# A streamed expert layer: single pieces early in the weight ring, and the second expert's first chunks ahead of the transposes

## The chip, the cores and the metric

The kernel runs on one core of one Trainium2 chip. The metric is the time of one execution on the device in microseconds (us); it is measured in several runs, of which the median is given. The profile is of one further execution.

## The reference

One layer of a streaming encoder on 512 frames of width 2048, in float32. The first part (norm, combined projection, chunked attention, short convolution, output projection) gives x. The second part, where the change lies, is a mixture of experts with hard routing:

```
glog, elog = xt @ w_rg + b_rg, xt @ w_re + b_re     # 4 groups, 32 experts in all
g_sel = argmax(glog);  top_v, top_i = top_k(elog of that group, 2)
w_tok = softmax(glog)[g_sel] * softmax(top_v)
...
a = silu(xblk @ w_gate[e]) * (xblk @ w_up[e])       # 2048 -> 512, for each expert e
y[tokens of e] += w_tok * (a @ w_down[e])           # 512 -> 2048
...
return rmsnorm(x + y, norm_final)
```

Every expert has 12.6 MB of weights (gate and up 8.4, down 4.2), 403 MB for all 32, and each is used once, by the few dozen tokens that picked it.

## The kernel before

**First part.** Up to about 800 us TensorE works through the dense projections and the attention; weights of the first two experts are fetched meanwhile. Then each token picks its experts (`choose`, `rank`), the experts are ordered by their number of tokens, and lists of token numbers are made.

**Units.** Experts are handled in units that share 128 slots: the first unit has the two experts with most tokens (by place in that order), 64 slots each; then a unit of four experts with 32 slots (a quarter unit); one full unit of two experts with 64 slots; two heavy units, whose first expert has 64 + 32 slots and whose second has 32; eight more full units; and a last quarter unit. For each unit the rows of its tokens are fetched from DRAM into one buffer, `xrow`, by an indirect DMA of POOL (L680), and turned by four steps (`turn_rows`, L687: four transposes each and a multiplication on DVE) into `xg`.

**One expert.** `gate_up` (L764) multiplies the slots with eight chunks of gate and up weights, accumulating in PSUM. `act1` (L773, L774; L778 to L782 for 32 slots) makes the activation on ACT and DVE, `act2` transposes it on TensorE (L788) and copies it (L790). `down` (L802) is the projection back with four chunks, whose results ACT and DVE write as a high and a low half, Yh and Yl (L808, L809).

**Combines.** The results of a unit go back to the token rows by multiplication with the unit's slot table. `slot_t` (L823) transposes the table; `comb` (L831, L832) are the 16 combines of a unit, each followed by an addition on DVE (L833). They stand in a list, `todo`, from which the next unit takes pieces to fill TensorE while its own work waits: 16 combines and then the four turns of the next unit's rows. How many are taken where is written in `plan`: a tuple for after each chunk of `gate_up`, then `gap` (ahead of the transposes of `act2`), `aft` (behind them) and `mid` (inside `down`). TensorE's order is as written; the other engines are ordered by the framework.

**The ring.** Weights pass through 14 places of 1 MB (`RING`). `loads` lists all pieces in order; `pump(n)` says that n more pieces will have been used and issues loads on the SP queue (L488, in `load_e`) for the places that this gives back. Before, two pieces are loaded by one DMA of 2 MB, except the last eight; such a load waits until both places are free. The order of the loads is that of use:

```
loads = [(u[i][0], c) for u in units for g in groups(u) for cs in (range(8), range(8, 12)) for i in g for c in cs]
```

**The first unit** is special: while its two `gate_up` run, `first(c)` and `second(c)` do the rest of the routing ahead of chunk c: fetching the rows for the second half of `xg`'s columns (`fetch_first`), picking rows by products with a selection (`first_gather`), counting and routing weights (`counts`, `weights`).

Of the kernel before, what the change touches and what calls it, by code (L numbers as in the profile page):

```python
# [10 lines left out]
F32 = mybir.dt.float32  # L11
# [8 lines left out]
P = 128  # L20
S = 512
# [8 lines left out]
SLOT = 64  # L30
NOV = 16
RING = 14
# [19 lines left out]
def tile_hymba_moe_layer(ctx, tc, xr, xT, smalls, wr, b3, wv, wt, wo, wgu, wd, out):  # L52
    nc = tc.nc

    def pool(stack, name, bufs=1, space=None, side="left"):
        kw = dict(name=name, bufs=bufs, reuse_waits="tile", side=side)
        if space is not None:
            kw["space"] = space
        return stack.enter_context(tc.tile_pool(**kw))
# [127 lines left out]
    fill = []  # L187
# [162 lines left out]
    for hb in range(4):  # L350
        us, ys = [], []
        ps = proj_t(8 + hb, FR)
        for c in range(2):
            u = ap.tile([P, S], F32, name="u", tag="u", bufs=2)
# [115 lines left out]
    chunks = {}  # L470
# [175 lines left out]
    for c, pl, tag, n in ((6, ylp, "Yl", 1), (7, wk, "xg", 2)):  # L646
        w = pl.tile([P, D], F32, name="w", tag=tag, bufs=n)
# [6 lines left out]
    psX = pool(ctx, "psX", space=PSUM)  # L654
# [17 lines left out]
    Sm = wk.tile([P, NT, 2 * SLOT], F32, name="Sm", tag="Sm", bufs=2)  # L672
    xg = wk.tile([P, KT, 2 * SLOT], F32, name="xg", tag="xg", bufs=2)
# [4 lines left out]
    def fetch_rows(ix, w):  # L678

        nc.gpsimd.indirect_dma_start(out=xrow[0:w, :], out_offset=None, in_=xd[:, :],  # L680
                                     in_offset=bass.IndirectOffsetOnAxis(ap=ix, axis=0),
                                     bounds_check=S - 1, oob_is_err=False)
# [14 lines left out]
    def token_of(dst, src, w):  # L697

        e = eye2[:, 0:NE]
        nc.vector.tensor_scalar(e[:, 0:w], src, 0.0, NONE, ALU.is_equal, ALU.mult)  # L700
        nc.vector.scalar_tensor_tensor(dst, src, -1.0, e[:, 0:w], ALU.add, ALU.add)
# [35 lines left out]
    def fetch_first():  # L737

        idp = psX.tile([P, 1], F32, name="idp", tag="dn", bufs=2)
        for t in range(NT):  # L740
            nc.tensor.matmul(idp, Sm[:, t, :], tok[:, t:t + 1], start=t == 0, stop=t == NT - 1)
        token_of(idx[:, 0:1], idp, 1)
        fetch_rows(idx[:, 0:1], P)
# [3 lines left out]
    def run(n):  # L747
        for _ in range(min(n, len(todo))):
            todo.pop(0)()

    def gate_up(xg, blocks, ch, fill, pre=None):
        pss = [psX.tile([P, S], F32, name="gu", tag="gx", bufs=3) for _ in blocks]
        for c in range(8):
            w = ch[c].rearrange("p (j g f) -> p j g f", j=2, g=2)
            if pre is not None:
                pre(c)
            for (n, o, _), ps in zip(blocks, pss):
                for j in range(2):  # L760
                    for g in range(2):
                        r = 64 * g if n == SLOT else 64 * j + 32 * g
                        q = 2 * c + j if n == SLOT else c
                        nc.tensor.matmul(ps[r:r + n, :], xg[:, 2 * c + j, o:o + n], w[:, j, g, :],  # L764
                                         start=q == 0, stop=q == (KT - 1 if n == SLOT else 7))
            run(fill if isinstance(fill, int) else fill[c])
        return pss
# [17 lines left out]
    def act2(n, a):  # L785
        tp = psM.tile([P, 4, n], F32, name="mp", tag="cb", bufs=3)
        for f in range(4):
            nc.tensor.transpose(tp[:, f, :], a[:, P * f:P * f + P], ident[0:n, 0:n])  # L788
        aT = wk.tile([P, 4, n], F32, name="aT", tag="aT", bufs=2)
        nc.scalar.copy(aT, tp)  # L790
        return aT
# [27 lines left out]
    def slot_t(Sm, w):  # L819

        tp = psM.tile([w, S], F32, name="mp", tag="cb", bufs=3)
        for t in range(NT):
            nc.tensor.transpose(tp[:, P * t:P * t + P], Sm[:, t, :], ident)  # L823
        ST = bt.tile([w, S], F32R, name="ST", tag="x1T", bufs=2)
        nc.vector.tensor_copy(ST, tp)  # L825
        return ST

    def comb(ST, Yh, Yl, w, t, db):
        sl = slice(S * db, S * db + S)
        cb = psM.tile([P, S], F32, name="cb", tag="cb", bufs=3)  # L830
        nc.tensor.matmul(cb, ST[:, P * t:P * t + P], Yh[0:w, sl], start=True, stop=False)  # L831
        nc.tensor.matmul(cb, ST[:, P * t:P * t + P], Yl[0:w, sl], start=False, stop=True)  # L832
        nc.vector.tensor_tensor(ACC[:, t, sl], ACC[:, t, sl], cb, ALU.add)  # L833

    def comb_units(Sm, Yh, Yl, w):
        box = []
        us = [lambda: box.append(slot_t(Sm, w))]
        for db in range(4):
            for t in range(NT):
                us.append(lambda t=t, db=db: comb(box[0], Yh, Yl, w, t, db))  # L840
        return us
# [115 lines left out]
    def first(c):  # L957
        if c in (4, 6):
            turn_rows(xg, P, 2 * c)
        if c == 1:  # L960
            fetch_first()
            for t in range(1, NT):
                first_gather(xps[1:2], 4, t)
        if c == 2:
            box["cntc"] = counts()
            box["rhs"] = weights()
        if c == 6:
            by_place(box["cntc"])
# [159 lines left out]
    def full(c, o):  # L1128
        return c, [(SLOT, o, c)]
# [8 lines left out]
    units = [[full(0, 0), full(1, SLOT)], Q[0], N[0], Hv[0], Hv[1]] + N[1:] + [Q[1]]  # L1138
# [7 lines left out]
    loads = [(u[i][0], c) for u in units for g in groups(u) for cs in (range(8), range(8, 12)) for i in g for c in cs]  # L1146
    loads = loads[:6] + loads[8:]

    loads[-8:] = [(u[0], c) for c in range(8, 12) for u in units[-1][2:]]
    regs = {}  # L1150

# [2 lines left out]
    def pump(n):  # L1154

        used[0] += n
        while nload[0] < len(loads):
            m = nload[0]
            w = 2 if m < len(loads) - 8 else 1
            if used[0] < m + w - RING:  # L1160
                break
            pos, c = loads[m]
            if pos < 2:
                e = slice(pos, pos + 1)
            else:
                if pos not in regs:
                    regs[pos] = nc.sync.value_load(ctl[0:1, pos:pos + 1], min_val=0, max_val=NE - 1)
                e = bass.ds(regs[pos], 1)
            chunks.setdefault(pos, []).extend(load_e(part(e, c, w), w))
# [4 lines left out]
    prev = []  # L1174
# [5 lines left out]
    def rcol(c):  # L1180
        return WRv[:, 1, c:c + 1]
# [17 lines left out]
    def step(p):  # L1199
        nonlocal cur, prev  # L1200
        Sm, xg, gu_ = cur
        cur = None
        todo.extend(prev)
        if p:
            cur = rows(p + 1)
            todo.extend([lambda g=cur[2], n=n: gather_to(g, n + 1) for n in range(4)])
        if p == 1:
            for j in range(len(HEAVY)):
                todo.insert(-4 * j - 2, lambda j=j: order_heavy(j))
        Yh, Yl = ytile()  # L1210

        def pre(c):
            gather_to(gu_, min(4, (c + c % 2) // 2 + 1))


        if p == 0:
            plan = [(0, 0, 0, 0)] * 2
        elif len(units[p]) == 4:
            plan = [(1, 0, 0, 0), (1, 3, 0, 0), (1, 2, 1, 0), (1, 2, 1, 0)]
        else:  # L1220
            plan = [((2, 2, 2, 2, 2, 2, 1, 1), 2, 0, 0), (1, 0, 0, 0)]
        turns = groups(units[p])
        left = len(units[p])
        for turn in turns:
            acts = []
            for i in turn:
                e, blocks = units[p][i]
                if p == 0:
                    pss = ps_first[i]
                    if i:  # L1230
                        order()
                        cur = rows(1)
                else:
                    pss = gate_up(xg, blocks, chunks[e], plan[i][0], pre)
                pump(8 if p or i else 6)
                acts.append([act1(n, ps, rcol(c)) for (n, _, c), ps in zip(blocks, pss)])
            for i, act in zip(turn, acts):
                e, blocks = units[p][i]
                _, gap, aft, mid = plan[i]
                left -= 1  # L1240
                if p == 0 and i:
                    gather_to(cur[2], 4)
                if left == 0:
                    gap = max(gap, len(todo) - aft - mid)
                run(gap)
                aTs = [act2(n, a) for (n, _, _), a in zip(blocks, act)]
                run(aft)
                if left == 0:
                    prev = comb_units(Sm, Yh, Yl, 2 * SLOT)
                    prev.pop(0)()  # L1250
                down([(n, o, aT, wcol(n, c)) for (n, o, c), aT in zip(blocks, aTs)], chunks[e], Yh, Yl, mid)
                pump(4)
        run(len(todo))
# [180 lines left out]
```

## Time and profile before

| what | value |
|---|---|
| median of 3 runs | 1802.97 us (1799.13 to 1803.94) |
| profiled execution | 1804.06 us, span 1802.4 us |
| TensorE busy | 1672.7 us (93%) |
| DVE, ACT, POOL busy | 770.6, 483.4, 81.2 us |
| mean granted TensorE clock | 0.966 of full |
| moved by DMA | 505.51 MB, mean 280 GB/s |

The span is the time from the first to the last instruction. Busy shares are means over stages with different limits; a TensorE that is busy is not at its peak, because matmuls overlap. A wait is given with what ended it.

### The profile page before, as it was taken

To read this page: it belongs to the slowest core of one execution; us is meant where nothing else is said; L and a number is where in the kernel's file an instruction comes from. 1 tells how busy PE (TensorE), PEld (TensorE's weight loads), DVE (VectorE), ACT (ScalarE), POOL (GpSimd) and SP (SyncE) were. 2 spreads that over 40 slices of the span, in tenths; PEclk is the share of its full clock that TensorE was granted. 3 is DMA by queue.
4 is the path that set the end of the run, shared out by engine and by line. 5 is a ranking of instruction groups with operands and counts; after the bars stand their busy time and mean duration, and the time that the engine had idled before them with its cause. 6 is when DMAs were issued, how large, how long until landed. Compare 5 with 4: busy or idle time off the path is not lost. (4 is left out here: it accounts for less than half of the span.)

```text
span 1802.4 us, 22250 instructions
## 1 busy us (share of the span) xinstructions
PE 1672.7 (93%) x9034; PEld 1012.6 (56%) x9034; DVE 770.6 (43%) x1427; ACT 483.4 (27%) x887; POOL 81.2 (5%) x91
## 2 busy tenths in 40 slices
PE   9999999999999999999876998889999999999974
PEld 7887777778888788774432333334444444443321
DVE  5236556542343633253543344443343334333446
ACT  6235555532222412330222112211111111111213
POOL 0000000011211200010000000000000000000000
PEclk9999999999999999989988999999999999999986
DMA  8222222232222635247999999899999999999995
GB/s 341 101 94 82 94 82 94 77 117 96 104 104 94 237 148 208 96 187 277 391 426 427 426 429 390 358 428 427 426 427 427 427 425 419 427 425 411 426 424 219
DMA packets 48187, 505.51 MB, mean 280 GB/s; under 512 B 6224, under 2 KB 6352, under 8 KB 12368
## 3 DMA queue, kind: packets, MB, share of 16 engines
q1 hardware_dynamic: 44784, 491.45, 66.8%
q0 software_dynamic: 3296, 12.59, 1.8%
q8 instruction: 73, 1.20, 0.3%
q14 instruction: 34, 0.28, 0.0%
HBM read 501.91 MB, written 8.39 MB: 283 GB/s over the span
## 5 line engine op out<-in xcount | busy, mean ns | idle before, releaser
L116 DVE TENSOR_TENSOR wlo<-raw,whi 128x1024 fp32r<-128x1024 f32 x126 | 159.1, 1266 | 281.1 <-ACT whi L115 280.3
L232 PE MATMUL pp<-hTh,whi 128*128 128x512 f32 x640 | 255.1, 399 | 0.0
L232 PE MATMUL pp<-hTl,whi 128*128 128x512 f32 x640 | 250.5, 391 | 0.0
L232 PE MATMUL pp<-hTh,wlo 128*128 128x512 f32 x640 | 250.4, 391 | 0.0
L833 DVE TENSOR_TENSOR X<-X,cb 128x512 f32<-128x512 f32 x224 | 146.6, 685 | 190.9 <-PE cb L832 190.2
L115 ACT CAST whi<-raw 128x1024 fp32r<-128x1024 f32 x126 | 132.2, 1051 | 336.9 <-PE pp L232 182.7
L764 PE MATMUL gu<-P,xg 128*64 128x512 f32 (+1 forms) x912 | 190.1, 615 | 12.9 <-DMA P<-in_wgu_dram 11.3
L809 DVE SCALAR_TENSOR_TENSOR Yl<-dn,WRv,Yh 64x256 fp32r<-64x256 f32 x176 | 85.1, 483 | 127.6 <-ACT Yh L808 127.4
L232 PEld LDWEIGHTS pp<-hTh,whi 128*128 128x128 f32 x640 | 120.5, 188 | 26.4 <-issue 3.9
L232 PEld LDWEIGHTS pp<-hTh,wlo 128*128 128x128 f32 x640 | 120.2, 188 | 25.2
L232 PEld LDWEIGHTS pp<-hTl,whi 128*128 128x128 f32 x640 | 120.4, 188 | 22.7 <-issue 0.7
L764 PE MATMUL gu<-R,xg 128*64 128x512 f32 (+1 forms) x624 | 124.9, 613 | 4.6 <-DMA R<-in_wgu_dram 4.6
L764 PE MATMUL gu<-ew,xg 128*64 128x512 f32 (+1 forms) x624 | 122.7, 620 | 3.5 <-DMA ew<-in_wgu_dram 3.5
L808 ACT ACTIVATE Yh<-dn,WRv 64x256 fp32r<-64x256 f32 x176 | 82.5, 469 | 139.4 <-PE dn L802 92.3
L773 ACT ACTIVATE sg<-gu,WRv 64x512 f32<-64x512 f32 x22 | 15.0, 683 | 382.6 <-PE gu L764 376.7
L802 PE MATMUL dn<-P,aT 128*64 128x256 f32 (+1 forms) x928 | 96.7, 418 | 14.9 <-DVE Yl L809 9.6
L831 PEld LDWEIGHTS cb<-Yh,ST 128*128 128x128 f32 (+1 forms) x224 | 42.2, 188 | 120.5 <-issue 85.2
L831 PE MATMUL cb<-Yh,ST 128*128 128x512 f32 (+1 forms) x224 | 103.2, 461 | 4.5 <-DVE ST L825 3.7
L764 PEld LDWEIGHTS gu<-P,xg 128*64 128x64 f32 (+1 forms) x912 | 47.3, 129 | 103.4 <-issue 86.4
L832 PE MATMUL cb<-Yl,ST 128*128 128x512 f32 (+1 forms) x224 | 89.0, 397 | 0.0
L802 PEld LDWEIGHTS dn<-P,aT 128*64 128x64 f32 (+1 forms) x928 | 53.6, 138 | 53.2 <-DVE Yl L809 16.4
L802 PE MATMUL dn<-R,aT 128*64 128x256 f32 (+1 forms) x576 | 66.8, 419 | 8.6 <-DVE Yl L809 4.0
(269 smaller groups left out, 2037.7 us busy)
## 6 DMA issues: line engine op xcount, KB each, us to landing
P<-in_wgu_dram SPq DMA_DIRECT2D x55, 2048.0 KB, 16.4
R<-in_wgu_dram SPq DMA_DIRECT2D x37, 2048.0 KB, 15.8
ew<-in_wgu_dram SPq DMA_DIRECT2D x35, 2048.0 KB, 15.7
P<-in_wd_dram SPq DMA_DIRECT2D x26, 2048.0 KB, 14.9
raw<-in_wt_dram SPq DMA_DIRECT2D x40, 1024.0 KB, 4.8
R<-in_wd_dram SPq DMA_DIRECT2D x17, 2048.0 KB, 16.7
ew<-in_wd_dram SPq DMA_DIRECT2D x17, 2048.0 KB, 14.6
raw<-in_wo_dram SPq DMA_DIRECT2D x16, 1024.0 KB, 5.0
```

The source lines that it names most:

```text
L115: nc.scalar.copy(hi, raw_slice)
L116: nc.vector.tensor_tensor(lo, raw_slice, hi.bitcast(F32), ALU.subtract)
L232: nc.tensor.matmul(ps[ct], w[bb][:, j, P * ct:P * ct + P], hT(a, kt), start=kt == 0 and n == 0, stop=kt == KT - 1 and n == 2)
L764: nc.tensor.matmul(ps[r:r + n, :], xg[:, 2 * c + j, o:o + n], w[:, j, g, :], start=q == 0, stop=q == (KT - 1 if n == SLOT else 7))
L773: nc.scalar.activation(sg, ps[0:64, :], AF.Silu, scale=rcol[0:64])
L802: nc.tensor.matmul(ps[n * q:n * q + n, :], aT[:, f, :], ws[db + q // 2][:, f, 256 * (q % 2):256 * (q % 2) + 256], start=f == 0, stop=f == 3)
L808: nc.scalar.activation(Yh[r0:r0 + n, c0:c0 + 256], src, AF.Copy, scale=wq)
L809: nc.vector.scalar_tensor_tensor(Yl[r0:r0 + n, c0:c0 + 256], src, wq, Yh[r0:r0 + n, c0:c0 + 256].bitcast(F32), ALU.mult, ALU.subtract)
L831: nc.tensor.matmul(cb, ST[:, P * t:P * t + P], Yh[0:w, sl], start=True, stop=False)
L832: nc.tensor.matmul(cb, ST[:, P * t:P * t + P], Yl[0:w, sl], start=False, stop=True)
L833: nc.vector.tensor_tensor(ACC[:, t, sl], ACC[:, t, sl], cb, ALU.add)
```

## The change

Five edits. The ring's pieces are loaded singly in the first two turns (28 pieces, of which 14 go through `pump`). In `first`, the picking of rows moves behind the second chunk's products, and the counting one chunk later. In units of two experts, full and heavy, the second expert's first two chunks are multiplied ahead of the first expert's transposes (`head`), and the loads are put in that order. The fills in `plan` are dealt out anew: 15 combines within the first expert's chunks and one behind its transposes; one turn of rows within the second expert's chunks, two ahead of its transposes together with the slot table, one behind. The slot table's copy out of PSUM goes from DVE to ACT.

```diff
-    def gate_up(xg, blocks, ch, fill, pre=None):
-        pss = [psX.tile([P, S], F32, name="gu", tag="gx", bufs=3) for _ in blocks]
-        for c in range(8):
+    def gate_up(xg, blocks, ch, fill, pre=None, part=range(8), pss=None):
+        if pss is None:
+            pss = [psX.tile([P, S], F32, name="gu", tag="gx", bufs=3) for _ in blocks]
+        for c in part:
...
-        nc.vector.tensor_copy(ST, tp)
+        nc.scalar.copy(ST, tp)
...
         if c == 1:
             fetch_first()
+        if c == 2:
             for t in range(1, NT):
                 first_gather(xps[1:2], 4, t)
-        if c == 2:
+        if c == 3:
             box["cntc"] = counts()
             box["rhs"] = weights()
...
+    for u in units[2:-1]:
+        i = loads.index((u[1][0], 0))
+        loads[i - 4:i + 2] = loads[i:i + 2] + loads[i - 4:i]
...
-            w = 2 if m < len(loads) - 8 else 1
+            w = 2 if 2 * RING <= m < len(loads) - 8 else 1
...
-            plan = [((2, 2, 2, 2, 2, 2, 1, 1), 2, 0, 0), (1, 0, 0, 0)]
+            plan = [((3, 2, 2, 2, 2, 2, 2, 0), 0, 1, 0), ((0, 0, 0, 0, 1, 0, 0, 0), 2, 1, 0)]
         turns = groups(units[p])
         left = len(units[p])
+        pair = p and left == 2
+        head = None
...
-                    pss = gate_up(xg, blocks, chunks[e], plan[i][0], pre)
-                pump(8 if p or i else 6)
+                    pss = gate_up(xg, blocks, chunks[e], plan[i][0], pre, range(2 if head else 0, 8), head)
+                pump(6 if head or not (p or i) else 8)
...
                     gap = max(gap, len(todo) - aft - mid)
+                    if pair:
+                        prev = comb_units(Sm, Yh, Yl, 2 * SLOT)
+                        prev.pop(0)()
                 run(gap)
+                if pair and left:
+                    e2, blocks2 = units[p][1]
+                    head = gate_up(xg, blocks2, chunks[e2], 0, None, range(2))
+                    pump(2)
                 aTs = [act2(n, a) for (n, _, _), a in zip(blocks, act)]
                 run(aft)
-                if left == 0:
+                if left == 0 and not pair:
```

## Rows read from the trace of the kernel before

**Rows 1.** Windows by stage: us, busy by engine, granted clock, DMA share, GB/s.
```profile
880.00:1080.00 200.00, 168.09 (x1096) 65.28 (x1092) 79.36 (x151) 34.67 (x72) 1.98 (x2) 0.91 1.00 426
...
1080.00:1120.00 40.00, 33.70 (x316) 15.29 (x320) 18.66 (x37) 13.02 (x28) 0.99 (x1) 0.96 0.95 387
1120.00:1160.00 40.00, 35.73 (x220) 14.14 (x212) 16.42 (x28) 6.36 (x14) 0.00 (x0) 0.96 0.91 380
1160.00:1200.00 40.00, 35.28 (x257) 14.48 (x258) 19.39 (x35) 8.91 (x19) 0.99 (x1) 0.91 0.96 398
...
1180.00:1500.00 320.00, 301.93 (x1668) 132.71 (x1662) 125.54 (x219) 51.76 (x108) 4.95 (x5) 0.97 1.01 427
1500.00:1700.00 200.00, 189.74 (x1062) 80.92 (x1059) 80.18 (x138) 30.13 (x62) 1.98 (x2) 0.98 1.00 421
```
**Rows 2.** One window of 5 us within the second heavy unit.
```profile
1155.00:1160.00 5.00, 3.81 (x48) 2.00 (x48) 2.50 (x6) 2.60 (x7) 0.00 (x0) 1.00 0.41 108
```
**Rows 3.** Timeline of the SP queue there: start, length, line, tile.
```profile
1157.02 0.33 SPq L488 DMA_DIRECT2D P<-in_wd_dram  x1
```
**Rows 4.** TensorE's waits in 1080 to 1200, then in 1200 to 1500: total, times, longest.
```profile
PE mp L788 <- DVE g2t L782: 11.4, 4, 3.0
...
PE mp L788 <- DVE a L774: 11.3, 10, 1.6
...
PE dn L802 <- ACT aT L790: 2.3, 5, 0.5
```
**Rows 5.** Timeline of TensorE in a full unit: start, length, [wait before].
```profile
1328.29 1.94 PE L764 MATMUL gu<-P,xg 128*64 128x512 f32 x8
...
1332.46 0.46 PE L788 MATMUL mp<-ident,a 64*128 64x64 f32 x4 [0.63 <-DVE a L774]
1333.38 3.67 PE L802 MATMUL dn<-P,aT 128*64 128x256 f32 x32 [0.46 <-ACT aT L790]
...
1340.94 1.89 PE L764 MATMUL gu<-R,xg 128*64 128x512 f32 x8
...
1350.71 7.09 PE L764 MATMUL gu<-ew,xg 128*64 128x512 f32 x32
1359.43 0.46 PE L788 MATMUL mp<-ident,a 64*128 64x64 f32 x4 [1.63 <-DVE a L774]
1359.82 0.66 PE L823 MATMUL mp<-ident,Sm 128*128 128x128 f32 x4
```
**Rows 6.** Timeline of TensorE in the second heavy unit, and the next unit's start.
```profile
1113.88 2.93 PE L764 MATMUL gu<-R,xg 128*64 128x512 f32 x16
...
1141.33 2.93 PE L764 MATMUL gu<-ew,xg 128*64 128x512 f32 x16
...
1149.32 5.32 PE L802 MATMUL dn<-P,aT 128*64 128x256 f32 x32
...
1164.58 1.04 PE L764 MATMUL gu<-P,xg 128*32 128x512 f32 x8
...
1172.62 1.90 PE L764 MATMUL gu<-ew,xg 128*32 128x512 f32 x16
1177.50 0.63 PE L788 MATMUL mp<-ident,g2t 32*128 32x32 f32 x4 [2.98 <-DVE g2t L782]
...
1184.80 1.94 PE L764 MATMUL gu<-P,xg 128*64 128x512 f32 x8
```
**Rows 7.** The first unit: timeline of TensorE and of the SP queue.
```profile
814.44 1.94 PE L764 MATMUL gu<-P,xg 128*64 128x512 f32 x8 [0.79 <-DVE xg L712]
...
869.68 3.46 PE L687 MATMUL xps<-ident,xrow 128*128 128x128 f32 x16 [5.50 <-DMA xrow<-xd,idx]
...
822.06 9.14 SPq L488 DMA_DIRECT2D P<-in_wd_dram  x3
...
860.11 17.99 SPq L488 DMA_DIRECT2D P<-in_wgu_dram  x3
```
**Rows 8.** Window in which the last single pieces come in.
```profile
1756.00:1768.00 12.00, 9.61 (x69) 4.15 (x73) 3.44 (x6) 2.30 (x5) 0.00 (x0) 0.54 1.02 421
```

## Prediction

> **What bounds the kernel.** I read the windows by stage first, because the weights pass through one ring and the question in each stage is whether the transfers or TensorE run out first. From 880 us on the DMA engines move 426 or 427 GB/s in the long quiet stretches and less in others [rows 1]. I take 427 as full rate; the time lost to idle transfers is then a stretch's length times the missing share: 200 x 1/427 = 0.5 us in 880 to 1080; 40 x 40/427 = 3.7 in 1080 to 1120; 40 x 47/427 = 4.4 in 1120 to 1160; 40 x 29/427 = 2.7 in 1160 to 1200; none in 1180 to 1500; 200 x 6/427 = 2.8 in 1500 to 1700. All later weights still have to come in, and the last expert's products wait for the last of them, so time is saved only where such an idle stretch is filled. The reader is to see two things in the same rows: TensorE is busy 302 of 320 us in 1180 to 1500, so it is nearly as full as the DMA, and DVE and ACT are far from full.
>
> Then I asked why the DMA idles at all. In 1155 to 1160 it moved 108 GB/s [rows 2], in the middle of the second heavy unit's projection back, and the queue issued its next pair at 1157.02 [rows 3], halfway through that projection: a new pair of pieces waits for the pair that held its place in the ring. So the transfers idle because TensorE releases pieces late, not for want of bandwidth. Last, the waits of TensorE: in both stretches asked, the longest are for the activation of the expert just multiplied (L788 behind DVE, L802 behind ACT) [rows 4], none for weights. These are the waits that the change fills.
>
> **A full unit, before and after** [rows 5]. The last chunk of the first expert ends at 1328.29 + 1.94 = 1330.2; three combines follow, then a wait of 0.63, transposes at 1332.46, a wait of 0.46, the projection back at 1333.38. A combine is (1332.46 - 0.63 - 1330.2) / 3 = 0.54 us, a chunk with nothing between 7.09 / 4 = 1.77, a slot table 0.66, and a row turn, four transposes of the same shape, as much. After: two more combines come before the last chunk (+1.1), then two chunks of the second expert (3.5), transposes (0.4), one combine (0.54). The activation needs what it needed before, 1332.46 - 1330.2 = 2.3 us, and the two chunks cover it; the combine covers ACT's 0.46. From the last chunk's old end to the projection: 1.1 + 3.5 + 0.4 + 0.5 = 5.5 instead of 3.2, that is 2.3 later, with 3.5 us of the second expert done. The second expert took 1359.82 + 0.66 - 1340.94 = 19.5 us to its projection. After: six chunks (10.6), one turn (0.66), slot table and two turns (2.3 against the wait of 1.63 that they fill; the last of these turns needs the PSUM buffer that the activation reads), transposes 0.4, one turn 0.66: about 14.6, 4.9 less. Net 4.9 - 2.3 = 2.6 us per full unit.
>
> That is worth little by itself. In 1180 to 1500 the DMA has no idle to give; TensorE would wait for weights instead. What these eight units can return is the 2.8 us of 1500 to 1700.
>
> **The heavy units** are where it pays [rows 6]. Take T = 1113.88, the start of the second one. Before, the last chunk of its first expert ends at 1141.33 + 2.93, T + 30.4, the projection runs from T + 35.4 to T + 50.7, and pairs of the ring come free at T + 30.4 (last gate pair), T + 43.1 (the issue at 1157.02), T + 50.7, then every 2.5 us or so. The transfers ran dry near T + 41 (1155). After, loads and uses have the second expert's first pair ahead of the projection. Two more combines precede the last chunk (+1.1); two half chunks take the 1.90 of 1172.62, so a pair comes free at about T + 33.3 instead of T + 43.1. That puts one transfer of 2.1 MB, 4.9 us at 427 GB/s, into the hole. The activations of the two blocks needed 1149.32 - 1144.26 = 5.1 us to the projection, with the additions of three combines between their steps on DVE; without these the chain is nearer the 3.0 that the half expert takes alone (1174.5 to 1177.50), so the projection starts near T + 35.2 and its pairs come free near T + 42.9 and T + 50.5. The DMA has work to about T + 50 and misses some 2 us instead of 4.4 + 2.7. The half expert shrinks too: 20.2 us from 1164.58 to 1184.80 become six chunks (5.7), a turn, the chain of 3.0 with slot table and turns inside it, transposes, a turn, and the same projection (5.7): about 16. A heavy unit is over 4 us shorter; the first passes that on to the second, less the 3.7 that the transfers themselves gain in the first. I take 10.5 of the 10.8 us as returned. The bounds: 4.9 if only one moved pair counts, and 10.8.
>
> **The front** [rows 7]. The first product ends at 814.44 + 1.94 = 816.4, but the ring's first pair is issued at 822.06, after the second. Single pieces, and the gather moved behind the second product, bring the first piece forward by 5.7 us and the second by about 3. What do they bring? The next pairs that count wait for the projections back (860.11, and the third of that row 17.99 after the first's start, near 878), the same 32 pieces are in by then either way, and the second projection waits for the next unit's gathered rows (5.50 us ending at 869.68). So the early start is lost unless those rows come sooner. Costs: the gather now stands right before the product that reads it, so its copy on DVE is exposed as at the first product, 0.79. Counting and routing weights go one product later; they are read at the seventh, so nothing. The row fetch may gain from queues emptied earlier: at most the 5.50, at least nothing; for the very first fetch, now beside early pieces, I allow 1 us. I take the sum as 0, between +2 and -4.
>
> On the size of pieces, the trace has eight queued single pieces of 1 MB carried at 421 GB/s in 1756 to 1768 [rows 8]. The Trainium skill (DMA: Bandwidth & Descriptors, section Bandwidth) gives 341 GB/s for a transfer of 1 MB measured by itself; by that, 14 pieces would need 43.0 instead of 34.4 us, and the sum would be up to 8.6 us worse. The trace disagrees for pieces that queue behind each other, and the sum goes by it.
>
> **Other edits.** The slot table's copy goes from DVE to ACT: ACT is busy 52 of 320 us, DVE 126 [rows 1]; the copy runs while DVE does the activation's product. Nothing, and at most 0.7, the length of the table itself, in the second expert. The last row turn is now near the unit's end, so POOL's next row fetch starts some 10 us later; its rows are first turned more than half a unit after that, so nothing, unless a fetch takes over 30 us.
>
> **Sum.** The profiled execution's own 1804.06 (span 1802.4 plus 1.7) - 10.5 - 2.8 - 0 = 1790.8. The median of the three runs is 1.1 lower, so I forecast 1790 us. A change under 0.3%, 5.4 us, can't be told from none here.
>
> **Rivals.**
> *The early start carries through.* The row fetch finds free queues, the 5.50 us wait goes nearly whole, and all later transfers move up by 4 to 5. Against it: the fetch still meets the pairs issued from 860.11 on. Time 1785.5, chance 0.10. The Trainium skill (Perfetto Trace Analysis, section DMA Optimizations) speaks for it: it advises splitting transfers so that some start sooner where the engines are idle. The idle is there before 822; whether it is worth anything, no row shows.
> *The hole moves.* The heavy unit's projection, 15 us with waits of its own, stays the late release; the moved pair is paid for by transfers that are late next, and less than half the gain is left: 2.8 + 2 = 4.8, less what the front may cost. Time 1797 to 1803, chance 0.13. That the edits fill waits of an engine that isn't the bound belongs here.
> *Slower: TensorE's clock.* Once full units wait for weights, the granted clock may fall to its lower level, 1.2 GHz, for part of each. In 880 to 1080 the granted mean was 0.91, against 0.97 in 1180 to 1500 [rows 1]. With 302 busy of 320 us at 0.97, a mean of 302 x 0.97 / 320 = 0.915 makes TensorE the bound again; to be 5.4 us slower in spite of the 10.5 it must stretch some 510 us by 16, 3.1%, a mean of 0.89. Against it: in 880 to 1080 the DMA stayed at 426 all the same, and a TensorE that falls behind stops waiting. At 0.88, stretched by 4%: 1790 + 20 + 3 = 1813; chance 0.04.
>
> **Chances.** Forecast 0.73, early start 0.10, hole 0.13, clock 0.04. Faster 0.83, same 0.13, slower 0.04. The range 1785 to 1797 leaves out the clock, most of the hole's case, and little else.
>
> **What would show it.** Right: over 415 GB/s in the heavy units' stretch; waits of L788 for DVE nearly gone; TensorE waiting for weights in the full units; the last weights landing some 13 us earlier; the first ring issue near 816.5. Wrong: a dip of the rate at the heavy units as deep as before, a second projection later than 880, or a granted clock under 0.9 in the full units with the rate below 420.

## The result, and the profile after

| | before | after |
|---|---|---|
| median, measured together | 1804.49 us | 1793.26 us (1788.44 to 1797.15, 6 runs) |
| ratio, 95% interval | | 0.9947 (0.9931 to 0.9964) |
| profiled execution | 1804.06 us, span 1802.4 | 1793.02 us, span 1791.3 |

The change makes the kernel faster by 9.6 us as the ratio has it, 11.2 by the medians, 11.1 between the two profiled spans. One of the six runs of the kernel before took 2398.04 us; the ratio leaves it out, and without it the medians differ by 10.7. Measured a second time, beside some of the experiments, it was 0.9955 (0.9939 to 0.9972), 8.1 us. The forecast was a gain of 13.3 us and a time of 1790, with a range of 1785 to 1797.

First the windows by stage, of the kernel after, for the stretches of [rows 1] and the hole of [rows 2]: us, busy time of PE, PEld, DVE, ACT and POOL, granted clock, DMA share, GB/s.

```profile
880.00:1080.00 200.00, 169.10 (x1126) 66.24 (x1120) 78.16 (x149) 35.72 (x75) 1.98 (x2) 0.91 1.01 426
1080.00:1120.00 40.00, 34.43 (x300) 15.22 (x300) 20.58 (x39) 12.42 (x27) 0.99 (x1) 0.96 1.01 426
1120.00:1160.00 40.00, 36.62 (x274) 14.44 (x270) 15.76 (x28) 9.36 (x20) 0.00 (x0) 0.96 0.99 419
1160.00:1200.00 40.00, 35.71 (x224) 15.05 (x222) 20.45 (x35) 7.29 (x15) 0.99 (x1) 1.00 1.01 426
1180.00:1500.00 320.00, 307.44 (x1719) 137.72 (x1720) 125.62 (x219) 53.30 (x111) 4.94 (x5) 1.00 1.01 426
1500.00:1700.00 200.00, 172.98 (x1068) 74.55 (x1064) 73.82 (x130) 36.34 (x76) 1.98 (x2) 0.99 1.01 427
1155.00:1160.00 5.00, 5.00 (x58) 1.87 (x56) 1.92 (x4) 2.06 (x5) 0.00 (x0) 0.84 0.93 377
```

The hole is gone: 426, 419 and 426 GB/s where there were 387, 380 and 398 [rows 1], and 377 in the five microseconds that had 108 [rows 2]. By the same reckoning as in the prediction, idle transfers cost 40 x (1 + 8 + 1)/427 = 0.9 us in 1080 to 1200 instead of 10.8, and nothing in 1500 to 1700 instead of 2.8.

Next the second heavy unit, as in [rows 6]: TensorE's timeline, then the SP queue's.

```profile
1106.96 2.93 PE L765 MATMUL gu<-R,xg 128*64 128x512 f32 x16
...
1138.11 1.90 PE L765 MATMUL gu<-P,xg 128*32 128x512 f32 x16
...
1142.29 3.67 PE L803 MATMUL dn<-P,aT 128*64 128x256 f32 x32
...
1157.54 2.75 PE L765 MATMUL gu<-R,xg 128*32 128x512 f32 x24
...
1172.50 1.94 PE L765 MATMUL gu<-P,xg 128*64 128x512 f32 x8
...
1140.07 0.33 SPq L488 DMA_DIRECT2D P<-in_wd_dram  x1
1148.34 9.78 SPq L488 DMA_DIRECT2D P<-in_wgu_dram  x2
```

With T = 1106.96, the half expert's first two chunks (1138.11, 1.90 us) are followed by a load at T + 33.1; the projection back starts at T + 35.3 and ends at T + 50.6, the unit takes 65.5 us instead of 70.9. The prediction had T + 33.3, T + 35.2, T + 50.5, and more than 4 us less.

TensorE's waits, in 1080 to 1200 (first two rows), in 1200 to 1500 (third) and in 1500 to 1690 (the rest): total, times, longest.

```profile
PE mp L789 <- DVE g2t L783: 6.7, 3, 2.9
PE dn L803 <- DVE Yl L810: 5.1, 4, 2.3
...
PE mp L789 <- DVE a L775: 2.2, 5, 0.4
...
PE gu L765 <- DMA P<-in_wgu_dram: 7.2, 6, 2.4
PE gu L765 <- DMA R<-in_wgu_dram: 5.3, 5, 1.8
PE gu L765 <- DMA ew<-in_wgu_dram: 4.4, 4, 1.6
```

In the full units the wait for the activation has gone from 11.3 to 2.2 us [rows 4], and TensorE waits for weights instead: 6.1 us in 1200 to 1500 and 16.9 in 1500 to 1690. In the heavy units 6.7 of 11.4 us are left, most of them in the half expert (2.9 us in each of the two units), whose own chain of steps nothing covers; they cost nothing, since the transfers run through.

Last the end of the kernel after: TensorE in the last unit, where gate chunks alternate with combines; then three rows of the kernel before.

```profile
1725.44 1.06 PE L765 MATMUL gu<-P,xg 128*32 128x512 f32 x8 [1.53 <-DMA P<-in_wgu_dram]
...
1728.27 1.93 PE L765 MATMUL gu<-P,xg 128*32 128x512 f32 x8
1730.13 0.79 PE L832 MATMUL cb<-Yh,ST 64*128 64x512 f32 x1
1730.72 0.62 PE L833 MATMUL cb<-Yl,ST 64*128 64x512 f32 x1
1731.28 1.94 PE L765 MATMUL gu<-P,xg 128*32 128x512 f32 x8
...
1746.35 1.43 PE L765 MATMUL gu<-R,xg 128*32 128x512 f32 x8
...
1752.01 6.50 PE L1313 MATMUL dn<-ew,aT 128*32 128x256 f32 x64
```

```profile
1726.03 1.90 PE L764 MATMUL gu<-ew,xg 128*32 128x512 f32 x8
...
1753.92 1.93 PE L764 MATMUL gu<-R,xg 128*32 128x512 f32 x8 [3.06 <-DMA R<-in_wgu_dram]
...
1763.51 5.61 PE L1298 MATMUL dn<-ew,aT 128*32 128x256 f32 x64
```

And the end of the transfers: two windows of the kernel after, then two of the kernel before (the last number is the rate).

```profile
1754.00:1757.00 3.00, 3.00 (x32) 1.34 (x28) 0.38 (x1) 0.47 (x1) 0.00 (x0) 0.50 0.72 300
1757.00:1760.00 3.00, 2.69 (x27) 1.21 (x19) 1.59 (x4) 1.19 (x3) 0.00 (x0) 0.94 0.22 93
...
1766.00:1769.00 3.00, 3.00 (x47) 1.39 (x39) 0.50 (x2) 0.94 (x2) 0.00 (x0) 0.82 1.02 415
1769.00:1772.00 3.00, 2.20 (x23) 1.12 (x24) 2.28 (x5) 1.54 (x4) 0.00 (x0) 1.00 0.55 224
```

Up to 1725 TensorE waits 1.53 us for each pair of chunks. Then the granted clock goes to half (0.50 in 1728 to 1744), its level of 1.2 GHz: a chunk takes 1.93 instead of 1.06 us, and a chunk with its combine 3.01 (1731.28 - 1728.27). A pair thus needs 6.0 us, while its 2.1 MB need 4.9 at 427 GB/s, and no further chunk waits for weights: in this execution TensorE sets the end. In the kernel before, TensorE was at the lower level for two chunks from 1726.03 on, but then back at the full one, and chunks still waited for weights up to the last but one (3.06 us ending at 1753.92); that chunk and the next ran at the lower level too. The transfers end some 13 us earlier than before (300 and 93 GB/s in the two windows from 1754 on, against 415 and 224 in those from 1766 on), the last projection starts 11.5 earlier (1752.01 against 1763.51), the span is 11.1 shorter.

### The profile page after: what moved, and what is told of

It is laid out like the page before. It is cut to its first block, busy times and chain, and to the rows that moved or that the text cites. A ratio compares the mean times of both kernels' runs of the same rounds, so it can differ in the third digit from the quotient of the medians.

```text
span 1791.3 us, 22282 instructions
## 1 busy us (share of the span) xinstructions
PE 1658.1 (93%) x9034; PEld 1007.3 (56%) x9034; DVE 759.3 (42%) x1413; ACT 490.7 (27%) x901; POOL 81.2 (5%) x91
## 5 line engine op out<-in xcount | busy, mean ns | idle before, releaser
L803 PE MATMUL dn<-P,aT 128*64 128x256 f32 (+1 forms) x896 | 92.7, 420 | 16.9 <-DVE Yl L810 12.5
L803 PE MATMUL dn<-R,aT 128*64 128x256 f32 (+1 forms) x608 | 63.4, 399 | 10.9 <-DMA R<-in_wd_dram 6.3
```

The source lines that it names most:

```text
L803: nc.tensor.matmul(ps[n * q:n * q + n, :], aT[:, f, :], ws[db + q // 2][:, f, 256 * (q % 2):256 * (q % 2) + 256], start=f == 0, stop=f == 3)
```

## The experiments

Ratios are to the kernel before, each measured on the same chip as its kernel, five rounds; the gain is (1 - ratio) times the median of before measured with it.

| kernel | median us | ratio, 95% interval | gain us |
|---|---|---|---|
| pairs_only | 1790.31 | 0.9935 (0.9920 to 0.9950) | 11.7 |
| front_only | 1804.12 | 1.0011 (0.9999 to 1.0022) | -2.0 |
| heavy_pairs | 1794.20 | 0.9960 (0.9945 to 0.9976) | 7.2 |
| full_pairs | 1799.65 | 0.9988 (0.9977 to 1.0000) | 2.2 |
| after_again | 1793.74 | 0.9955 (0.9939 to 0.9972) | 8.1 |
| st_vector | 1792.82 | 0.9949 (0.9932 to 0.9966) | 9.2 |
| tail_busy | 1793.44 | 0.9944 (0.9929 to 0.9960) | 10.1 |
| tail_stack | 1790.65 | 0.9938 (0.9921 to 0.9955) | 11.2 |
| before_stack | 1802.76 | 0.9992 (0.9983 to 1.0001) | 1.4 |
| stack_pairs | 1790.99 | 0.9933 (0.9919 to 0.9946) | 12.1 |
| no_shift | 1790.73 | 0.9921 (0.9908 to 0.9935) | 14.2 |
| stack_no_shift | 1788.57 | 0.9920 (0.9902 to 0.9937) | 14.4 |

The first four ran on one chip, the next four in the table on a second, the next three on a third; the last was run later, on that third chip too. An interval reaches 2 to 3 us to either side, so differences of less than some 4 us between two kernels are not settled by one pair of them. Comments behind # in the diffs below are for the reader only.

### Which part brings the gain

**pairs_only** undoes the front:

```diff
-            w = 2 if 2 * RING <= m < len(loads) - 8 else 1
+            w = 2 if m < len(loads) - 8 else 1
...
-        if c == 2:
             for t in range(1, NT):
                 first_gather(xps[1:2], 4, t)
-        if c == 3:
+        if c == 2:
             box["cntc"] = counts()
```

> The changed kernel with its front undone (ring's first turns in pairs, the first expert's projection carrying its extra work at the old chunks), so only the second expert's early chunks, the earlier slot table, the scalar copy of it and the new load order are left. Theory (the gain is the idle time of the transfers at the heavy units, about 10 us, and in the full units, 2.8 us; the front is worth at most the 2.7 us by which the second projection came earlier): 1794 to 1797 us against 1793.3 for the whole change, 426 GB/s kept in 1080 to 1200. Rival (the early start carries through to the end): the whole lead of 5.74 us of the first ring transfer is lost, 1798 us or more.

**front_only** puts just these edits into the kernel before (the same lines, the other way round).

> The kernel before with the front edits alone: single pieces in the ring's first two turns, and the first expert's projection with its gather and its routing work one chunk later. Theory: 1801 to 1804 us against 1804.5, at most the 2.7 us of the second projection, and the dip of the transfer rate at the heavy units is still there (under 200 GB/s in some 5 us, 380 to 400 in 1120 to 1200). Rival (early start carries through): 1799 us or less.

**heavy_pairs** and **full_pairs** give the new order to some units only:

```diff
+    paired = (3, 4)     # full_pairs: every unit of two experts but these
-    for u in units[2:-1]:
+    for u in [units[p] for p in paired]:
...
+        elif p not in paired:
+            plan = [((2, 2, 2, 2, 2, 2, 1, 1), 2, 0, 0), (1, 0, 0, 0)]
...
-        pair = p and left == 2
+        pair = p in paired
```

> The changed kernel, but only the two heavy units have the new order (second expert's first chunks, slot table, next rows, load order); the full units have the old plan and the old order of loads. Theory: most of the gain is made in the heavy units, so 1794 to 1798 us, 425 GB/s or more in 1080 to 1200, about 421 in 1500 to 1700. Rival (the gain is spread over all units with two experts, so 2 of 14 such units bring a seventh of it): 1801 to 1804 us.

> The opposite half: full units in the new order, the two heavy units in the old one. Theory: 1799 to 1803 us, the dip at the heavy units as deep as before (380 to 400 GB/s in 1120 to 1200), 427 in 1500 to 1700. Rival (gain spread over all units): 1794 to 1797 us.

Without the front the gain is all there, 11.7 us; at 1790.31 us the kernel is even faster than the 1794 to 1797 that were expected. The front by itself, single pieces and shifted work together, gains nothing, and its ratio leans to slower. So the early start doesn't carry through in the changed kernel. Nor is the gain spread evenly over the units: two heavy ones bring 7.2 us and nine full ones 2.2. The windows say why; first heavy_pairs:

```profile
1120.00:1160.00 40.00, 36.62 (x267) 14.79 (x270) 16.02 (x28) 9.16 (x19) 0.00 (x0) 0.96 1.00 423
1500.00:1700.00 200.00, 188.33 (x1122) 81.61 (x1124) 77.62 (x133) 36.24 (x74) 1.98 (x2) 0.98 1.00 420
```

and full_pairs:

```profile
1120.00:1160.00 40.00, 34.79 (x212) 14.00 (x212) 16.39 (x29) 7.21 (x15) 0.00 (x0) 0.96 0.87 362
1500.00:1700.00 200.00, 177.44 (x1070) 76.53 (x1064) 73.23 (x127) 35.38 (x73) 1.99 (x2) 1.00 1.01 427
```

and front_only, which has the old order in all units:

```profile
1120.00:1160.00 40.00, 34.77 (x217) 14.10 (x218) 16.33 (x28) 7.21 (x15) 0.00 (x0) 0.96 0.92 382
1500.00:1700.00 200.00, 189.09 (x1078) 80.91 (x1074) 79.51 (x137) 33.09 (x68) 1.98 (x2) 0.98 1.00 425
```

Each half fills its own idle stretch and leaves the other's about as it was [rows 1]. How much there is to fill differs between executions, in the full units above all: the four profiles with these in the old order moved 420 to 425 GB/s in 1500 to 1700, which is 3.3 to 0.9 us of idle transfers. (pairs_only kept 425 and 423 in 1080 to 1160, but 407 in 1160 to 1200.) Both halves contain the front. Against front_only, on the same chip, the heavy units' part is worth 1801.9 x (1.0011 - 0.9960) = 9.2 us and the full units' 1801.9 x (1.0011 - 0.9988) = 4.1, each give or take some 3.

### The front

Where does the early start go? The second unit waits for its gathered rows [rows 7]. Below are POOL's fetch of these rows (in brackets its wait since the fetch before) and the transposes that wait for them, in pairs_only:

```profile
856.21 0.99 POOL L680 DMA_INDIRECT xrow<-xd,idx  x1 [36.50 <-DVE w L1295]
...
869.02 3.67 PE L687 MATMUL xps<-ident,xrow 128*128 128x128 f32 x16 [5.05 <-DMA xrow<-xd,idx]
```

in the kernel after:

```profile
857.38 0.99 POOL L680 DMA_INDIRECT xrow<-xd,idx  x1 [37.59 <-DVE w L1296]
...
868.32 2.10 PE L687 MATMUL xps<-ident,xrow 128*128 128x128 f32 x16 [3.19 <-DMA xrow<-xd,idx]
```

and in stack_no_shift, which has the single pieces, but the first expert's work at its old chunks:

```profile
855.26 0.99 POOL L680 DMA_INDIRECT xrow<-xd,idx  x1 [36.49 <-DVE w L1307]
...
865.97 3.43 PE L687 MATMUL xps<-ident,xrow 128*128 128x128 f32 x16 [2.95 <-DMA xrow<-xd,idx]
```

Two effects with opposite signs can be read. From the fetch's issue to its use it is 12.8 us here with pairs (12.5 to 13.8 in the four profiles with pairs in these turns) and 10.7 to 10.9 with single pieces (10.7 to 11.9 in ten profiles): the rows are there 1 to 2 us sooner. Whether the size of the pieces does that, or that they were issued earlier, no run separates. But the work put one chunk later makes the fetch itself 1.1 us later: 36.5 us after the one before in all four profiles with pairs and in stack_no_shift, 37.6 to 37.8 in all eight with singles and the shift. TensorE's timeline shows where: from the start of the first product to the row turn behind the fourth it takes 12.38 us in the kernel after and in front_only, 11.29 in pairs_only and 11.28 in stack_no_shift. So the shift takes back most of what the single pieces give. That led to **no_shift**:

```diff
-        if c == 2:
             for t in range(1, NT):
                 first_gather(xps[1:2], 4, t)
-        if c == 3:
+        if c == 2:
             box["cntc"] = counts()
```

> The changed kernel with single pieces in the ring's first two turns, but the first expert's projection with its gather and routing work at the old chunks. Theory (the two front edits are worth nothing, each for itself as together): 1791 to 1795 us, 0.994 to 0.9955. Rival (the later gather costs about 1 us and the single pieces bring it back): 1 to 2 us faster than the whole change, 0.9935 or less.

It gained 14.2 us, at the rival's end and beyond it. **stack_no_shift** tried it again later, together with an edit of the last unit told below:

> Single pieces in the ring's first two turns, the first expert's work at the old chunks, the pair edits, and the one-product combines of the last unit. Theory (the front's edits are worth nothing, and the 0.9921 of the kernel with the work at the old chunks was chance, since its trace shows nothing in the front that is earlier): 0.9925 to 0.994, as the two other kernels with these combines. Rival (the work one chunk later does cost 2 to 3 us, in a way that the one trace doesn't show): 0.989 to 0.9915.

14.4 us, between the two expectations, with an interval that reaches into both. Taken together, the kernels with all the pair edits gained 8.1 to 11.2 us with singles and shift (four kernels, one of them measured twice), 11.7 and 12.1 with neither, 14.2 and 14.4 with singles alone. The order is the one that the traces give, but the steps are larger: the shift would cost 4 to 5 us, while the traces show 1.1. In the profile of no_shift itself, its slowest execution (span 1793.3), the fetch came even 37.91 us after the one before. That is TensorE's clock and not the edit. Below is the first product, in no_shift and then in stack_no_shift, which has the same front:

```profile
812.68 3.68 PE L765 MATMUL gu<-P,xg 128*64 128x512 f32 x8 [0.78 <-DVE xg L712]
...
813.29 1.94 PE L765 MATMUL gu<-P,xg 128*64 128x512 f32 x8 [0.78 <-DVE xg L712]
```

The granted clock was 0.50 in 812 to 816 and 0.58 in 816 to 822 in no_shift, and 1.00 in both in all thirteen other profiles; the stretch of 11.28 us took 15.26. So that profile can't speak against the 1.1, but no profile shows the other 3 to 4 us either. Whether they are chance, a difference of chips or times, or something that one profile doesn't show, stays open.

### The last unit

The profile after says that TensorE at its lower clock level sets the end of that execution. **tail_stack** takes work from it: the first two quarter blocks' high and low halves are put on top of each other, so that a combine is one product, not two.

```diff
-            down([(32, 32 * i, act2(32, a), wcol(32, c))], chunks[c], Yh, Yl, 0)
+            down([(32, 32 * i, act2(32, a), wcol(32, c))], chunks[c], Yh, Yh, 0, SLOT)   # low half from row 64 on
...
-        todo.extend(comb_units(Sm[:, :, 0:SLOT], Yh, Yl, SLOT))
+        todo.append(slot_t1)                     # the table twice over, as slot_t2 makes it
+        todo.extend([lambda t=t, db=db: comb1(t, db) for db in range(4) for t in range(NT)])
...
+            nc.tensor.matmul(cb, box["ST1"][:, P * t:P * t + P], Yh[:, sl], start=True, stop=True)
```

> The changed kernel, but in the last unit the first two quarter blocks' results are put with their upper and lower parts on top of each other in one tile, as the last two already are, so each of the 16 combines in the last eight pairs of chunks is one matrix product, not two (the table is built twice over for it). Theory (after the change TensorE sets the end: from 1725 us on it is at the lower clock level and takes 3.01 us for a chunk with its combine, 6.0 for a pair whose weights come in 4.9): a combine falls from 1.1 to 1.4 us to about 0.6 to 0.8, a pair to about 5, and the end comes 1.5 to 3 us sooner, 1790 to 1792 us. Rival (the end is set by the last weights' landing): no change, 1793 to 1794 us.

**tail_busy** does the opposite: it makes each of these combines' products twice.

```diff
+        if w == SLOT and twice:                  # only in the last unit's second half
+            nc.tensor.matmul(cb, ST[:, P * t:P * t + P], Yh[0:w, sl], start=True, stop=False)
+            nc.tensor.matmul(cb, ST[:, P * t:P * t + P], Yl[0:w, sl], start=False, stop=True)
```

> The changed kernel, but the combines between the last two quarter experts' chunks make each matrix product pair twice (the first result is written over), 32 products more of about 0.33 us at the full level, in a stretch in which TensorE waits 1.53 us in every 4.9 for weights. Theory A (the granted level falls at 1725 us because TensorE had stood waiting so much): the full level is kept, TensorE goes on waiting for weights to the last chunk, and the end comes 1 to 2 us sooner, 1791 to 1792 us. Theory B (the level falls at about that time whatever TensorE does there): at the lower level the extra work adds about 1 us to each of some eight to ten chunks, 1800 us or more.

**st_vector** puts `slot_t`'s copy back on DVE (`nc.vector.tensor_copy(ST, tp)`), and **after_again** is the changed kernel itself.

> The changed kernel with one edit undone: the slot table's copy out of PSUM goes back from ScalarE to VectorE. Theory: within 0.5 us of the whole change (1792.8 to 1793.8), since TensorE waits for weights in the full units and none of these copies is on the path there; in the last unit the wait of 3.66 us for this copy that the kernel before shows comes back, and lies at the start of a stretch that waits for weights anyway. Rival: that wait delays the last combines, 1 to 3.7 us slower than the whole change.

> The changed kernel as it is, on the same chip as the three others, as their measure: 1793.3 us, 0.9947 of the kernel before.

In tail_stack's trace the mechanism is plain:

```profile
1730.30 1.06 PE L765 MATMUL gu<-P,xg 128*32 128x512 f32 x8 [1.75 <-DMA P<-in_wgu_dram]
1731.29 0.71 PE L1301 MATMUL cb<-Yh,ST 128*128 128x512 f32 x1
1731.94 1.94 PE L765 MATMUL gu<-P,xg 128*32 128x512 f32 x8
...
1736.74 1.06 PE L765 MATMUL gu<-R,xg 128*32 128x512 f32 x8 [2.14 <-DMA R<-in_wgu_dram]
```

The clock still falls (1.94 us at 1731.94), but TensorE has time to spare and waits 2.14 us for the next weights. In time it gained 3.1 us on after_again (0.0017 of 1802.6), with an uncertainty of some 4.

tail_busy decides neither way. In its trace chunks stay at the full level, and wait for weights, up to 1734, later than in the kernel after; then it falls all the same:

```profile
1734.11 1.07 PE L766 MATMUL gu<-P,xg 128*32 128x512 f32 x8 [1.33 <-DMA P<-in_wgu_dram]
...
1736.63 1.94 PE L766 MATMUL gu<-P,xg 128*32 128x512 f32 x8
...
1740.49 1.93 PE L766 MATMUL gu<-R,xg 128*32 128x512 f32 x8
```

That execution, at 3.9 us a chunk (1740.49 - 1736.63), took 1800.1 us; another of the same kernel took 1790.4. So neither "busy keeps the clock" nor "it falls in any case" is shown; the place where it falls and rises differs from one execution to the next.

st_vector is the same as the whole change within the interval, as expected; the wait of 3.66 us for the table's copy, which was to come back, is not in its profile. Its profiled execution (1790.67 us) was one of its shorter ones, and shows what the clock costs: there the chunks were back at the full level from 1738 on.

```profile
1738.55 1.07 PE L765 MATMUL gu<-R,xg 128*32 128x512 f32 x8
...
1742.93 1.07 PE L765 MATMUL gu<-R,xg 128*32 128x512 f32 x8 [1.01 <-DMA R<-in_wgu_dram]
...
1749.62 0.62 PE L1313 MATMUL dn<-ew,aT 128*32 128x256 f32 x2
```

TensorE catches up with the weights, the last projection starts at 1749.62 instead of 1752.01, and the span is 1789.0 instead of 1791.3.

The last question was whether the shorter combines help only where the change has made TensorE the bound. **before_stack** has them in the kernel before (the diff of tail_stack), **stack_pairs** in pairs_only.

> The kernel before with the last unit's combines made as one matrix product each (the edit that is worth about 3 us on the changed kernel). Theory (before the change TensorE waits for weights up to the last chunks, so its own time in that stretch is not what ends last; the change turned that round): within 1 us of the kernel before, ratio 0.9995 to 1.0005. Rival (the edit shortens the last unit whatever goes before it, through its fewer products and its smaller table): 2 to 3 us faster here too, ratio 0.998 or 0.9985.

> The changed kernel without its front edits and with the one-product combines of the last unit: what the runs so far point to as the fastest. Theory (the front is worth nothing, the combines 3 us): 0.9925 to 0.994 of the kernel before, 1788.5 to 1791.5 us, the same as with the front within what can be measured. Rival (the front is worth 2.7 us once the end is set by the weights' landing again): 0.995 or more.

Here my account of the time falls short. On the kernel before the edit gains 1.4 us (-0.2 to 3.1), between both expectations; on pairs_only it gains 0.0002, on no_shift 0.0001, that is nothing. The three comparisons on changed kernels give 3.1, 0.4 and 0.2 us, 1.2 on average, no more than on the kernel before. That TensorE sets the end of the changed kernel in some executions is shown by the traces: after its level fell, no chunk of the last unit waits for weights in the profiles of the kernel after, after_again and pairs_only. In that of no_shift, with the same instructions there, TensorE was back at the full level by 1734 and then waited again:

```profile
1742.04 1.44 PE L765 MATMUL gu<-R,xg 128*32 128x512 f32 x8 [2.89 <-DMA R<-in_wgu_dram]
```

That TensorE's level costs 3 us in the median is not shown.

The fastest version run is stack_no_shift, 1788.57 us, 14.4 us below the kernel before; no_shift, which needs fewer edits, is not distinguishable from it.

## Why the prediction was right, and where it was off

**The bound** was read rightly: transfers idle because TensorE releases ring places late, and time is saved only where that idle is filled. heavy_pairs and full_pairs show it stretch by stretch. One reading was incomplete: TensorE's second longest wait, L802 behind DVE's Yl (5.0 us in 1080 to 1200, 3.6 in 1200 to 1500), is longer than the one behind ACT that the prediction names. It lies inside the projection back, and the change leaves it: 5.1 and 4.2 us.

**The heavy units**, 10.5 us: 9.2 measured against front_only, give or take 3, and 9.9 us of the 10.8 idle filled. The steps behind it (T + 33.3, T + 35.2, T + 50.5) came within 0.2 us. One of the times on the way was off: the load after the projection's first part came at T + 41.4, not T + 42.9. The lower bound of 4.9 was too cautious.

**The full units**, 2.8 us: 4.1 measured, with an uncertainty of some 3; the idle of 1500 to 1700 was filled whole, and the wait moved from the activation to the weights as described. What the combines and turns gain in a full unit was rightly held to be worth nothing more, TensorE being idle afterwards. That 9.2 and 4.1 add up to just the 13.3 of the forecast is luck: one was forecast too high and the other too low, each within its uncertainty, and the 2.8 was read from one execution, where others have 0.9 to 3.3.

**The front**, taken as 0 between +2 and -4, is the term that was mis-sized: +2.0 us (-0.2 to +4.0) by front_only, and 2 to 4 by pairs_only against the whole change. That is the upper end of the stated bounds, and its interval reaches zero. The parts were named: the exposed copy was put at 0.79 and delays the fetch by 1.1; what the row fetch gains was put between nothing and 5.50 and is 1 to 2 us, which didn't pay for the shift in the measured times. Here the Trainium skill (Perfetto Trace Analysis, section DMA Optimizations) gave the rival: split transfers may start sooner where the engines are idle. They did, by 5.8 us (816.28 against 822.06), and the traces agree with the rule as far as the gathered rows. The wait for them did not go nearly whole, as the rival had it: 2.9 to 4.2 us of it are left in the ten profiles with single pieces. With the shift the end of the kernel did not move; without it, single pieces are 2.5 and 2.3 us ahead of pairs (no_shift against pairs_only, stack_no_shift against stack_pairs), which is within the uncertainty.

**The size of pieces.** The Trainium skill (DMA: Bandwidth & Descriptors, section Bandwidth) has 341 GB/s for a transfer of 1 MB, issued from GpSimd, where the pieces here are issued from SP. The prediction's sum ruled such a cost out; the front's traces do not: in 857 to 861, where four single pieces had just been queued, the transfers ran at 326 to 354 GB/s in nine of the ten profiles with single pieces (399 in the tenth), and at 360 to 418 in the four with pairs. The gathered rows pass in the same stretch, and the transfers were less busy just before it (306 GB/s in 851 to 857 in the kernel after, 365 in the kernel before), so the size isn't isolated. What follows did not come later for it: the third load of the pairs after them waits for places that the projection back frees, and was issued at 874.0 to 878.3 us in nine of the ten (879.6 in no_shift), against 877.9 to 879.1 with pairs.

**What the sum left out** is the last unit. Idle that is filled earlier reaches the end only if TensorE can follow, and in the profiled execution it could not quite: transfers ended some 13 us earlier, the last projection started 11.5 earlier. The prediction had the clock as a rival, but looked for it in the full units, where the granted mean was 0.99 to 1.00. Of the 13.3 forecast, the pair edits measured 11.7 by themselves (9.0 to 14.4) and the whole 8.1 and 9.6; the front accounts for about 2 of the difference, and the rest is inside the intervals.

**The slot table's copy and the later row fetch** cost nothing that could be measured, as said: st_vector is 0.9949 against 0.9947 and 0.9955, and in 1180 to 1500 the transfers ran at 426.

## What to carry to other kernels

Where a ring of buffers feeds from DRAM at full rate, look for the stretches in which the rate dips, and ask which buffer's release is late; moving one early use ahead of a long block of other work can fill the hole, and doing the same in stretches without a dip only turns one wait into another. Before adding up what filled holes are worth, check that the consumer at the very end can follow an earlier last transfer. An earlier start at the front is worth what the next thing that gates the work lets through, and work moved to make room for it may cost more than it brings.

## What the runs showed of the hardware

The indirect gather of 128 rows took 10.7 to 11.9 us from issue to use in the ten profiles in which the weights queued just before it were pieces of 1 MB, and 12.5 to 13.8 in the four in which they were pairs of 2 MB. The pieces were also issued earlier, so what the size alone does is not shown.

TensorE's granted clock in the last unit does not follow from that unit's instructions alone. They are the same in the kernel after, where it fell to its lower level near 1726 us and stayed there to the last gate chunk at 1746, and in no_shift, where it fell near 1725, was back by 1734 and fell once more from 1742 to 1746. The engine had been waiting for weights for part of each pair of chunks before it fell, 1.53 and 1.51 us, in both. The two profiles of the kernel after itself agree: in after_again it fell in the same chunk and was back in the same one.

The spread between executions of one kernel, 1788.4 to 1797.2 us for the kernel after, is as large as most of the effects that this study set out to separate.
